# The second mixer of a two-layer trunk: gate rows read from masked tables in DRAM in place of broadcasts on TensorE

## The chip, the core and the metric

The kernel runs on one core of one Trainium2 chip. A core has TensorE (matrix products, rows PE, its weight loads PEld), VectorE (DVE), ScalarE (ACT), GpSimd (POOL), SyncE (SP, which here only issues transfers) and 16 DMA engines. Each engine works through its own instructions in a fixed order; semaphores tie them together. Products land in PSUM, everything else lies in SBUF, 128 partitions wide, or in DRAM. The metric is the device time of one execution in microseconds (us).

## The reference

Two layers of a bidirectional trunk run over 128 context tokens and 512 latent tokens, 1024 wide, with the same weights. The first layer mixes tokens by a gated delta rule and attention, the second by an mLSTM; each is followed by a gated feed-forward. The change is in the second mixer. Its recurrence, for each of 8 heads and both directions, is

```python
    log_d = jnp.where(incl, b[..., :, None] - b[..., None, :] + log_i[..., None, :], -jnp.inf)
    def step(carry, inp):
        m_t = jnp.maximum(m_in, m_intra_c)
        w_inter = jnp.exp(m_in - m_t)
        s = qk_c * jnp.exp(log_d_c - m_t[..., None])
        num = w_inter[..., None] * jnp.einsum('bhtk,bhkv->bhtv', q_c, C) + jnp.einsum('bhts,bhsv->bhtv', s, v_c)
        den = w_inter * jnp.einsum('bhtk,bhk->bht', q_c, nv) + jnp.sum(s, axis=-1)
        h = num / jnp.maximum(jnp.abs(den), jnp.exp(-m_t))[..., None]
```

What matters here: the exponent of `s` is a sum of a term of the key position s, a term of the query position t (call it the gate row, one value per t), and a mask that is 0 or very negative. `w_inter` is the exponential of another piece of the same gate row. Afterwards `h` is normalised, gated and multiplied by `ml_w_out`.

## The kernel before

All of it is one Tile program, `tile_trunk`. The 640 tokens are 5 tiles of 128. Products in fp32 are made of three passes over values split into a high and a low part; the weights come in by SP's transfers (`wr`), are cast on ScalarE (`wh`, L477) and the rest is made on VectorE (`wl`, L478). Thirty SBUF slots of 128 x 1296 are handed out in turn (`U.get`, `U.put`); a transfer into a slot waits until its last reader is done. `later` is a queue of deferred pieces of work, of which `tick(n)` runs n. The program's text gives the order only in outline: a scheduler decides at build time in which order each engine gets its instructions.

The second mixer, `layer1`, projects token by token in five chunks (`gemm_tok`, `in_w_ml`, to about 1098 us). Behind the first chunk `gates` makes, on a few partitions, `r2f`, the gate rows of 8 heads and 2 directions over 640 tokens, and their exponentials in partitions 64 to 127. Both are split into `r2h` (a cast, L1654) and `r2l` (the difference, L1655).

Then come ten units, in the order context unit 0, latent 0 to 3, context unit 1, latent 4 to 7. A latent unit is one head and four tiles of 128 tokens; a context unit is four heads and one tile. For each unit `weights` makes `qk` (L1743), and for each direction the exponent `bc` in PSUM: one product with the identity puts the mask there (L1749), and one each with `r2h` and `r2l` adds the gate row to all 128 partitions (L1754; four narrow ones each in a context unit). For latent units `qb` is the exponential row on all partitions (L1759, L1760), which VectorE multiplies into the queries (`mqs`, L1762). ScalarE takes four exponentials `me` of `bc` with the key's term `colA` as bias (L1766), and VectorE multiplies by `qk` (L1768). `outputs` makes `num` and `numb` from these (L1783, L1786), the normaliser `rn` on VectorE, `hs` in two halves (ScalarE L1803, VectorE L1805), squares `jk` on ScalarE (L1809) and the reciprocal root `mrs` on POOL (L154). `store` applies it (L1821), transposes on TensorE (`ht`, L1823) and splits the result. A unit's `weights` stand ahead of the `outputs` of the unit before. From unit 5 on the output projection `op` (L502) is laid between the units. Before the first unit's outputs come the state updates of all chunks (`ktok`, `wk`, `mst` L1718, `st` L1724).

Of the kernel before, what the change touches and what calls it, by code (L numbers as in the profile page):

```python
# [11 lines left out]
F32 = mybir.dt.float32  # L12
# [73 lines left out]
def tile_trunk(ctx: ExitStack, tc: tile.TileContext, A, dbg=None, stop=None):  # L86
# [402 lines left out]
    def tick(n=1):  # L489

        for _ in range(min(n, len(later))):
            later.popleft()()
# [32 lines left out]

    def gemm_tok(x, units, kk, n, evac, depth=3, fill=0, fills=None):

        ga, gb, mm_ = g_tile("tka"), g_tile("tkb"), m_tile("tkm")
        accs = [ga[:, 0:512], ga[:, 512:1024], gb[:, 0:512], gb[:, 512:1024], mm_[:, :]]
        for u in range(units):  # L530
# [18 lines left out]
            if u < units - 1:  # L549
                tick(2)  # L550

# [164 lines left out]
    def ffn_s(l, nm, xt, xs, xd, done):  # L716
# [27 lines left out]
        with tc.tile_pool(name=f"wp{l}", bufs=2, side="right") as rp:  # L744
# [38 lines left out]

            hid = {}

# [8 lines left out]
            for f in range(CLASSIC, NF, 2):  # L794
                last = f == NF - 2
                gate = None
                for which in range(2):
# [3 lines left out]
                    def then(n):  # L801
                        if end and n == 0:
                            W.until = len(wspecs) if l else w_layer1
                            W.fetch(2)
                        if end:
                            for _ in range(2):
                                if coming[0] < THIRDS[0][1]:
                                    hid_in(coming.popleft())
                        else:
                            step(STEPS[min(unit, 3)][n], todo)  # L810
                        if n == 5 and unit >= 3 and ada_todo:
                            ada_fill(1)
                            ada_load(1)
# [662 lines left out]


    def layer1(nm, xt, xs, xd):
        with ExitStack() as lay:
# [43 lines left out]

            gt = sm([NT, 32], "gt")
            vsl = [U.get("v1") for _ in range(4)]
# [28 lines left out]

            r2h, r2l = sm([T], "r2h", F32R), sm([T], "r2l", F32R)
            dec = sm([NT], "dec")
# [5 lines left out]
            def gates():  # L1562
                gls = U.get("gl")
                gl = gls[:, :1280].rearrange("p (t a r) -> p t a r", t=NT, a=4)
                pool.memset(gls[:, :1280], 0.0)
                fx, fa = sm([NT, 16], "fx"), sm([NT, 16], "fa")
                dve.tensor_tensor(out=fx, in0=gt[:, :, 16:32], in1=fb[:, None, :].to_broadcast([P, NT, 16]), op=ALU.add)
# [24 lines left out]
                for j in range(4):  # L1592
                    for d in range(2):
                        src = 1 + (j if d == 0 else 3 - j)
                        pe.matmul(pi[0:64, 512 + P * j:640 + P * j], lhsT=gl[:, src, 2 + d, :], rhs=sl[d][:, 896:1024],
                                  start=d == 0, stop=d == 1)
                U.put(gls, *sl)
                br = U.get("br")
# [54 lines left out]
                act.activation(br[64:128, 648:648 + T], br[0:64, 648:648 + T], AF.Exp)  # L1653
                act.copy(r2h, r2f)  # L1654
                dve.tensor_tensor(out=r2l, in0=r2f, in1=r2h.bitcast(F32), op=ALU.subtract)  # L1655
                act.activation(ra[64:128], ra[64:128], AF.Exp)
# [32 lines left out]
            for c in range(1, 5):  # L1689
                for i in sorted({hh // 2 for kind, hh, _, _ in ML_CHUNKS[c] if kind == "o"} - set(ogs)):  # L1690
                    ogs[i] = U.get("og")
                    ogv[i] = ogs[i][:, :1280].rearrange("p (t h d) -> p t h d", t=NT, h=2)
                gemm_tok(h, 4, 2, 416, evac(ML_CHUNKS[c]), 3, fill=1 if len(ada_todo) > 8 else 0)
                next(pieces, None)
                next(pieces, None)
            h.put()


# [39 lines left out]
            def weights(items):  # L1738
# [5 lines left out]
                hh = items[0][0]  # L1744
                bc = g_tile("bc")
                qs, ss = [], []
                for d in range(2):
                    bd = bc[:, 512 * d:512 * d + 512]
                    pe.matmul(bd, lhsT=ident_r, rhs=mneg_r[:, d, None, :].to_broadcast([P, 4, P]), start=True, stop=False)  # L1749
                    rows = [(hh, slice(0, 512), slice(TP, T))] if lat else [  # L1750
                        (h_, slice(i * P, i * P + P), slice(0, TP)) for i, (h_, c) in enumerate(items)]
                    for part in (r2h, r2l):
                        for i, (h_, o, src) in enumerate(rows):
                            pe.matmul(bd[:, o], lhsT=ident_r[:, 32 * d + h_:32 * d + h_ + 1].to_broadcast([P, P]),  # L1754
                                      rhs=part[:, src], start=False, stop=part is r2l and i == len(rows) - 1)
                    if lat:
                        qb = m_tile("qb")
                        row = ident_r[:, 64 + 32 * d + hh:65 + 32 * d + hh].to_broadcast([P, P])
                        pe.matmul(qb, lhsT=row, rhs=r2h[:, TP:T], start=True, stop=False)  # L1759
                        pe.matmul(qb, lhsT=row, rhs=r2l[:, TP:T], start=False, stop=True)  # L1760
                        q_ = t_tile("mqs")
                        dve.tensor_tensor(out=q_[:, :512], in0=qb, in1=qp[hh][:, TP:T], op=ALU.mult)  # L1762
                        qs.append(q_)
# [4 lines left out]
                    dve.tensor_tensor(out=e[:, :512], in0=e[:, :512], in1=pq, op=ALU.mult)  # L1768
                    ss.append(e)
                return qs, ss  # L1770

            def outputs(items, qs, ss):
# [73 lines left out]
            def finish(u):  # L1846
                store(order[u], *hss.pop(u))
                hh, c = order[u][0]
                if c and hh % 2:
                    U.put(vsl[hh // 2], ogs[hh // 2], qsl[hh // 2])  # L1850
                    if hh % 4 == 3:
                        U.put(ksl[hh // 4])

            wts[0] = weights(order[0])
            pt = ktok(0)
            wks = deque(wkeys(0, d, pt) for d in range(2))
            steps = [(1 + n if d == 0 else 4 - n, d, n) for n in range(3) for d in range(2)]
            for i in range(8):
# [11 lines left out]
                if i == 5:  # L1870
                    wts[1] = weights(order[1])
            U.put(cps)
            W.until = len(wspecs)
            for u in range(1, len(order)):
                if u + 1 < len(order):
                    wts[u + 1] = weights(order[u + 1])
                finish(u - 1)
                if u == 5:
# [174 lines left out]
```

## Time and profile before

| | us |
|---|---|
| runs | 1692.59, 1695.3, 1696.57 |
| median | 1695.3 |
| profiled execution | 1693.63 |
| its span in the profile | 1691.9 |
| TensorE busy | 1636.2 (97%) |
| VectorE busy | 1229.7 (73%) |
| ScalarE busy | 763.0 (45%) |

The span is what the trace covers; the execution's own time is 1.7 longer. An engine's busy time is the time in which it had an instruction under way, so a share of the span is an average over stages that have different limits. For TensorE the starts of successive matmuls tell more than their durations, which overlap. A wait is shown with what released the engine.

### The profile page before, as it was taken

What the parts mean: (1) busy time and instruction counts of PE and PEld (TensorE: products, weight loads), DVE (VectorE), ACT (ScalarE), POOL (GpSimd) and SP (SyncE); (2) the same over time, 40 slices, a digit from 0 to 9 for tenths busy, and PEclk for the clock granted to TensorE, in tenths of its full rate; (3) what the DMA queues carried; (4) which work ended last, traced back from release to release, by engine and by line L of the source; (5) the groups of instructions that cost most, each with busy time, mean ns of one, the idle gap of its engine ahead of it and who ended that gap; (6) DMA issues with size and microseconds to landing.
All of it is one profiled execution on the core that took longest, in us unless ns stands there. A gap on an engine that the chain in (4) does not pass through costs nothing. (4 is left out here: it accounts for less than half of the span.)

```text
span 1691.9 us, 28080 instructions
## 1 busy us (share of the span) xinstructions
PE 1636.2 (97%) x10896; PEld 1561.8 (92%) x10896; DVE 1229.7 (73%) x2354; ACT 763.0 (45%) x1646; POOL 149.6 (9%) x243
## 2 busy tenths in 40 slices
PE   7999988998999999999999999999999999999998
PEld 3799776798999999999999989978999999999998
DVE  7788977777888888978855755377677988865432
ACT  5784255564455444442224623246455534443210
POOL 0000024641000000000001000001010000000000
PEclk9999999999999999999999999999999999999999
DMA  8232611105621544467532434401240444338221
GB/s 337 92 101 83 198 45 29 29 13 161 233 90 66 169 148 158 147 212 276 202 99 98 155 88 158 151 28 57 92 164 24 137 167 142 118 109 308 88 76 63
DMA packets 80653, 216.21 MB, mean 128 GB/s; under 512 B 20196, under 2 KB 21348, under 8 KB 80520
## 3 DMA queue, kind: packets, MB, share of 16 engines
q1 hardware_dynamic: 75720, 194.75, 35.1%
q0 software_dynamic: 4800, 19.66, 3.0%
q8 instruction: 86, 1.41, 0.3%
q14 instruction: 47, 0.39, 0.1%
HBM read 186.85 MB, written 27.53 MB: 127 GB/s over the span
## 5 line engine op out<-in xcount | busy, mean ns | idle before, releaser
L502 PE MATMUL fd<-hid,wh 128*128 128x320 f32 x1408 | 264.5, 309 | 0.0
L477 ACT CAST wh<-wr 128x1024 fp32r<-128x1024 f32 (+4 forms) x148 | 134.1, 912 | 275.5 <-DMA wr<-in_w_d 131.6
L502 PEld LDWEIGHTS fd<-hid,wh 128*128 128x128 f32 x1408 | 220.9, 188 | 0.0
L692 PE MATMUL sb<-ht,ph 128*128 128x320 f32 x1008 | 199.3, 311 | 0.7 <-DVE ht L614 0.5
L478 DVE TENSOR_TENSOR wl<-wr,wh 128x1024 fp32r<-128x1024 f32 (+3 forms) x116 | 133.3, 1152 | 87.2 <-ACT wh L477 62.1
L692 PEld LDWEIGHTS sb<-ht,ph 128*128 128x128 f32 x1008 | 160.5, 188 | 3.0 <-DVE ht L614 0.8
L502 PE MATMUL fd<-hid,wl 128*128 128x320 f32 x704 | 160.2, 309 | 0.0
L318 DVE SCALAR_TENSOR_TENSOR aj<-ar,cs 128x1024 bf16<-128x1024 f32 x112 | 133.7, 1220 | 24.9 <-DMA ar<-in_ada_w 24.9
L692 PE MATMUL sad<-hb,ph 128*128 128x320 f32 x576 | 128.1, 309 | 0.0
L502 PEld LDWEIGHTS fd<-hid,wl 128*128 128x128 f32 x704 | 118.0, 188 | 0.0
L502 PE MATMUL op<-mxh,wh 128*128 128x320 f32 x512 | 99.0, 312 | 1.1 <-DVE xc L554 1.0
L554 DVE SCALAR_TENSOR_TENSOR xd<-fd,mod,xd 128x128 f32<-128x128 f32 x96 | 48.4, 546 | 66.6 <-PE fd L502 66.5
L692 PEld LDWEIGHTS sad<-hb,ph 128*128 128x128 f32 x576 | 96.4, 188 | 0.0
L652 DVE TENSOR_TENSOR pl<-s,ph 128x1024 fp32r<-128x1024 f32 x72 | 88.0, 1222 | 4.1 <-ACT ph L651 3.6
L692 PE MATMUL sad<-hb,pl 128*128 128x320 f32 x288 | 88.9, 309 | 0.0
L692 PE MATMUL sb<-ht,pl 128*128 128x320 f32 x288 | 88.7, 308 | 0.0
L651 ACT CAST ph<-s 128x1024 fp32r<-128x1024 f32 x72 | 75.2, 1049 | 27.3 <-PE fg L502 8.9
L502 PEld LDWEIGHTS op<-mxh,wh 128*128 128x128 f32 x512 | 80.9, 188 | 2.0 <-ACT rh L216 1.2
L651 ACT CAST ph<-wp 128x1024 fp32r<-128x1024 f32 (+1 forms) x72 | 60.0, 835 | 41.5 <-PE sad L692 22.8
L692 PE MATMUL sad<-ht,ph 128*128 128x320 f32 x288 | 64.9, 313 | 1.3 <-DVE c L703 1.1
L652 DVE TENSOR_TENSOR pl<-wp,ph 128x1024 fp32r<-128x1024 f32 x36 | 44.0, 1221 | 29.1 <-issue 21.1
L692 PE MATMUL sb<-hn,ph 128*128 128x320 f32 x288 | 64.8, 309 | 0.0
(551 smaller groups left out, 3997.1 us busy)
## 6 DMA issues: line engine op xcount, KB each, us to landing
ar<-in_ada_w SPq DMA_DIRECT2D x61, 512.0 KB
wp<-in_w_g SPq DMA_DIRECT2D x36, 512.0 KB
wp<-in_w_u SPq DMA_DIRECT2D x36, 512.0 KB
wr<-in_w_d SPq DMA_DIRECT2D x32, 512.0 KB
hf<-hd SPq DMA_DIRECT2D x44, 320.0 KB
hd<-c POOLq DMA_DIRECT2D x36, 320.0 KB, 2.5
adas<-in_ada_w SPq DMA_DIRECT2D x19, 512.0 KB
wr<-in_w_ml SPq DMA_DIRECT2D x20, 416.0 KB
```

The costliest lines, as they stand in the source:

```text
L318: dve.scalar_tensor_tensor(out=junk, in0=st, scalar=one, in1=ada["cs"][:, s, :], op0=ALU.mult, op1=ALU.mult, accum_out=mod[l][q][:, s, j:j ...
L477: act.copy(hi, raw[:, :n])
L478: dve.tensor_tensor(out=lo, in0=raw[:, :n], in1=hi.bitcast(F32), op=ALU.subtract)
L502: pe.matmul(ps[:, LO + a:LO + b], lhsT=wv[:, k, :], rhs=xk[:, a:b], start=k == 0 and p_ == 0, stop=k == kk - 1 and p_ == 2)
L554: dve.scalar_tensor_tensor(out=x[:, a:b], in0=ps[:, LO + a:LO + b], scalar=gate[:, s, j:j + 1], in1=x[:, a:b], op0=ALU.mult, op1=ALU.add)
L651: act.copy(hi, src)
L652: dve.tensor_tensor(out=lo, in0=src, in1=hi.bitcast(F32), op=ALU.subtract)
L692: pe.matmul(bank[o], lhsT=wv[:, k, :], rhs=xv, start=o not in seen and k == 0 and p_ == 0, stop=k == 3 and p_ == 2, skip_group_check=True)
```

## The change

A generator `masks` runs in the first feed-forward, at most one step in each of its units 3 to 14: it loads the mask once, spreads it over 128 x 1024 on VectorE and stores it into ten tables `mb` in DRAM, 512 KB each. In `gates` the split is gone; eight transfers on SP store the latent gate rows (`rl`), their exponentials (`re`) and the context rows (`rc`) in DRAM, and ten `add_row` are put on `later`: each is a transfer on POOL's queue that reads a row on all 128 partitions and adds it to a table in DRAM. `gemm_tok` takes one piece of `later` after each weight tile in the last four chunks where it took two. `weights` has no products for `bc` and `qb` left: the exponentials read the table from a slot `mbt`, the queries are multiplied by `qbt`, and `load_rows` brings both in, two units ahead. The small gate tiles move to a slot `gx`. Names in the new kernel: its L1743 is L1774, L1766 is L1786, L1783 and L1786 are L1816 and L1819.

```diff
@@ gemm_tok
-    def gemm_tok(x, units, kk, n, evac, depth=3, fill=0, fills=None):
+    def gemm_tok(x, units, kk, n, evac, depth=3, fill=0, fills=None, ticks=2):
...
-                tick(2)
+                tick(ticks)
@@ ffn_s
-            hid = {}
+            hid, masking = {}, masks()
...
+                        if n == 3 and l == 0 and 3 <= unit < 15:
+                            next(masking, None)
@@ new, ahead of layer1
+    def masks():
+
+        r = U.get("mrep")
+        m_ = v3(r[:, 1024:1280], 2)
+        sp.dma_start(out=m_, in_=A["mneg"])
+        dve.tensor_copy(r[:, :1024].rearrange("p (d c t) -> p d c t", d=2, c=4), m_.unsqueeze(2).to_broadcast([P, 2, 4, P]))
+        yield
+        for i in range(10):
+            mb.append(dram.tile([P, 2 * TS], F32, name=f"mb{i}"))
+            sp.dma_start(out=mb[i], in_=r[:, :1024])
+            yield
+        U.put(r)
+
@@ layer1, gates
-            r2h, r2l = sm([T], "r2h", F32R), sm([T], "r2l", F32R)
+            rl, re = (dram.tile([8, 2 * TS], F32, name=n) for n in ("rl", "re"))
+            rc = dram.tile([2, 2, 4, TP], F32, name="rc")
...
-                act.copy(r2h, r2f)
-                dve.tensor_tensor(out=r2l, in0=r2f, in1=r2h.bitcast(F32), op=ALU.subtract)
+                for d in range(2):
+                    r8, t_ = slice(32 * d, 32 * d + 8), slice(TS * d, TS * d + TS)
+                    sp.dma_start(out=rl[:, t_], in_=r2f[r8, TP:T])
+                    sp.dma_start(out=re[:, t_], in_=br[64 + 32 * d:72 + 32 * d, 648 + TP:648 + T])
+                    for g_ in range(2):
+                        sp.dma_start(out=rc[g_, d], in_=r2f[32 * d + 4 * g_:32 * d + 4 * g_ + 4, 0:TP])
+
+                def add_row(i):
+                    row = rl[i:i + 1, :] if i < 8 else rc[i - 8].rearrange("d i t -> (d i t)").unsqueeze(0)
+                    pool.dma_start(out=mb[i], in_=row.to_broadcast([P, 2 * TS]), accum_op=ALU.add)
+
+                later.extend(lambda i=i: add_row(i) for i in (8, 0, 1, 2, 3, 9, 4, 5, 6, 7))
@@ layer1, after the gates
-                gemm_tok(h, 4, 2, 416, evac(ML_CHUNKS[c]), 3, fill=1 if len(ada_todo) > 8 else 0)
+                gemm_tok(h, 4, 2, 416, evac(ML_CHUNKS[c]), 3, fill=1 if len(ada_todo) > 8 else 0, ticks=1)
...
             h.put()
+            tick(len(later))
@@ weights
-                bc = g_tile("bc")
+                mbt, qbt = rows.popleft()
                 qs, ss = [], []
                 for d in range(2):
-                    bd = bc[:, 512 * d:512 * d + 512]
-                    pe.matmul(bd, lhsT=ident_r, rhs=mneg_r[:, d, None, :].to_broadcast([P, 4, P]), start=True, stop=False)
-                    rows = [(hh, slice(0, 512), slice(TP, T))] if lat else [
-                        (h_, slice(i * P, i * P + P), slice(0, TP)) for i, (h_, c) in enumerate(items)]
-                    for part in (r2h, r2l):
-                        for i, (h_, o, src) in enumerate(rows):
-                            pe.matmul(bd[:, o], lhsT=ident_r[:, 32 * d + h_:32 * d + h_ + 1].to_broadcast([P, P]),
-                                      rhs=part[:, src], start=False, stop=part is r2l and i == len(rows) - 1)
+                    bd = mbt[:, TS * d:TS * d + TS]
                     if lat:
-                        qb = m_tile("qb")
-                        row = ident_r[:, 64 + 32 * d + hh:65 + 32 * d + hh].to_broadcast([P, P])
-                        pe.matmul(qb, lhsT=row, rhs=r2h[:, TP:T], start=True, stop=False)
-                        pe.matmul(qb, lhsT=row, rhs=r2l[:, TP:T], start=False, stop=True)
                         q_ = t_tile("mqs")
-                        dve.tensor_tensor(out=q_[:, :512], in0=qb, in1=qp[hh][:, TP:T], op=ALU.mult)
+                        dve.tensor_tensor(out=q_[:, :512], in0=qbt[:, TS * d:TS * d + TS], in1=qp[hh][:, TP:T], op=ALU.mult)
...
                     ss.append(e)
+                U.put(mbt)
                 return qs, ss
+            rows = deque()
+            def load_rows(items):
+                hh, c = items[0]
+                mbt, qbt = U.get("mb"), None
+                sp.dma_start(out=mbt[:, :2 * TS], in_=mb[hh if c else 8 + hh // 4])
+                if c:
+                    qbt = hq.tile([P, 2 * TS], F32, tag="qb", bufs=2, name="qb")
+                    sp.dma_start(out=qbt, in_=re[hh:hh + 1, :].to_broadcast([P, 2 * TS]))
+                rows.append((mbt, qbt))
 
@@ units
+            load_rows(order[0])
+            load_rows(order[1])
             wts[0] = weights(order[0])
...
                 if i == 5:
                     wts[1] = weights(order[1])
+                    load_rows(order[2])
...
                     wts[u + 1] = weights(order[u + 1])
+                if u + 2 < len(order):
+                    load_rows(order[u + 2])
```

What the scheduler made of it on three engines follows, of before and of the changed kernel.

TensorE, at one of the last latent units, behind a piece of the output projection (`wh`, `mxh` and `mxl` belong to it); before:

```order
L1743 MATMUL qk<-qp_9543,kp_10087 128x128 x4
L1749 MATMUL bc<-mneg_r,ident_r 128x512
L1754 MATMUL bc<-r2h,ident_r 128x512
L1754 MATMUL bc<-r2l,ident_r 128x512
L1759 MATMUL qb<-r2h,ident_r 128x512
L1760 MATMUL qb<-r2l,ident_r 128x512
L1759 MATMUL qb<-r2h,ident_r 128x512
L1760 MATMUL qb<-r2l,ident_r 128x512
L1783 MATMUL num<-v_573_9893,me 128x129
L1786 MATMUL num<-st_11164,mqs 128x129
```

and now:

```order
L502 MATMUL op<-mxh_680_11211,wh_12002 128x320 x2
L1774 MATMUL qk<-qp_9567,kp_10111 128x128 x4
L1816 MATMUL num<-v_576_9917,me 128x129
L1819 MATMUL num<-st_11202,mqs 128x129
L1816 MATMUL num<-v_576_9917,me 128x129
```

The seven products of the mask, the gate row and the exponential rows between `qk` and the first `num` are gone, and the three in the second direction too.

ScalarE, at the end of the projections (`og` are gate evacuations out of the accumulators `tkb`, `tkm`); before:

```order
L1548 ACTIVATE og_10817<-tkm 128x128
L1546 ACTIVATE og_11004<-tkm 128x256
L1548 ACTIVATE og_10414<-tkm 128x32
L1766 ACT_TABLE_LOAD
L1766 ACTIVATE me<-bc,colA 128x128 x8
L1721 COPY cp_11170<-mst 128x258 x4
```

and now, where `mb_11213` is the slot with the table of context unit 0:

```order
L1566 ACTIVATE og_10442<-tkb 128x32
L1786 ACT_TABLE_LOAD
L1786 ACTIVATE me<-mb_11213,colA 128x128
L1566 ACT_TABLE_LOAD
L1566 ACTIVATE og_10851<-tkb 128x128
L1564 ACTIVATE og_11041<-tkb 128x256
L1566 ACTIVATE og_10442<-tkb 128x32
L1566 ACTIVATE og_10851<-tkm 128x128
L1564 ACTIVATE og_11041<-tkm 128x256
L1566 ACTIVATE og_10442<-tkm 128x32
L1786 ACT_TABLE_LOAD
L1786 ACTIVATE me<-mb_11213,colA 128x128 x7
```

One exponential, which reads the loaded table, now stands ahead of the last six evacuations, with a load of the function table on either side; the seven others stand behind them, with a third.

POOL, behind the gates (`gl`, `br`, `cb` are tiles of the gates, `mrs` the reciprocal roots of the mixer); before:

```order
L1565 MEMSET gl_10144 128x1280
L1624 MEMSET br_10240 128x640
L1603 MEMSET cb_10242 64x64
L1603 MEMSET cb_10243 64x64
L1603 MEMSET cb_10244 64x64
L154 TENSOR_TENSOR mrs<-msq,mhalf 128x4 x10
```

and now, `mb8` and `mb9` being the tables of the context units and `mb0` to `mb7` those of the heads:

```order
L1623 MEMSET cb_604_10266 64x64
L1683 DMA mb8_7286<-rc_10105 128x1024
L1683 DMA mb9_7416<-rc_10105 128x1024
L1683 DMA mb0_6237<-rl_10103 128x1024
L1683 DMA mb1_6367<-rl_10103 128x1024
L1683 DMA mb2_6499<-rl_10103 128x1024
L1683 DMA mb3_6629<-rl_10103 128x1024
L1683 DMA mb4_6761<-rl_10103 128x1024
L1683 DMA mb5_6891<-rl_10103 128x1024
L1683 DMA mb6_7023<-rl_10103 128x1024
L1683 DMA mb7_7154<-rl_10103 128x1024
L154 TENSOR_TENSOR mrs_11362<-msq_11345,mhalf_87 128x4
```

The ten additions stand in a row on POOL's queue between the gates and the mixer. On SP seven of the ten stores of the masks stand in a row between two pairs of the first feed-forward's weight loads (`in_w_g`, `in_w_u`), three behind; and seven table loads stand where loads of the residual (`xc`) were, near the end of the projections.

## Rows read from the trace of the kernel before

**Rows 1.** The page, busy times of the engines and the granted clock in 40 slices

```profile
PE 1636.2 (97%) x10896; PEld 1561.8 (92%) x10896; DVE 1229.7 (73%) x2354; ACT 763.0 (45%) x1646; POOL 149.6 (9%) x243
...
PEclk9999999999999999999999999999999999999999
```

**Rows 2.** Windows: length; PE, PEld, DVE, ACT, POOL busy; clock; DMA share; GB/s

```profile
1098.10:1116.60 18.50, 17.48 (x172) 13.78 (x171) 11.52 (x34) 9.12 (x34) 0.10 (x1) 1.00 0.19 65
1116.60:1166.00 49.40, 45.02 (x333) 39.56 (x332) 36.92 (x111) 28.95 (x109) 4.94 (x5) 1.00 0.09 28
1166.00:1217.50 51.50, 51.50 (x374) 49.71 (x373) 37.38 (x110) 25.25 (x93) 5.34 (x5) 1.00 0.13 42
1217.50:1247.20 29.70, 28.71 (x193) 28.16 (x193) 22.68 (x43) 16.56 (x27) 3.66 (x7) 1.00 0.74 257
```

**Rows 3.** Waits from 1116.6 to 1166.0 us: total us, times, longest

```profile
ACT me L1766 <- PE bc L1754: 13.0, 6, 3.9
PEld num L1783 <- ACT jk L1809: 4.1, 4, 1.7
ACT hs L1803 <- DVE rn L1797: 3.8, 4, 1.5
```

**Rows 4.** Timeline of PE, first matmuls of two units: start, us, what

```profile
1128.99 1.06 PE L1743 MATMUL qk<-qp,kp 128*128 128x128 f32 x8
...
1137.10 1.05 PE L1743 MATMUL qk<-qp,kp 128*128 128x128 f32 x8
```

**Rows 5.** Timeline of PE, around the gate rows of a latent unit

```profile
1166.81 0.48 PE L1749 MATMUL bc<-mneg_r,ident_r 128*128 128x512 f32 x1
...
1168.52 0.38 PE L1783 MATMUL num<-v,me 128*128 128x129 f32 x2
...
1169.77 0.47 PE L1749 MATMUL bc<-mneg_r,ident_r 128*128 128x512 f32 x1
...
1170.54 0.38 PE L1783 MATMUL num<-v,me 128*128 128x129 f32 x2
```

**Rows 6.** Timeline of PE, a direction of the first context unit

```profile
1098.93 0.47 PE L1749 MATMUL bc<-mneg_r,ident_r 128*128 128x512 f32 x1
...
1100.09 1.06 PE L1731 MATMUL ktok<-cm,kp 128*128 128x128 f32 x8
```

**Rows 7.** Timeline of ACT, the first exponentials of the mixer

```profile
1099.32 1.28 ACT L1766 ACT_TABLE_LOAD   x1
1100.61 1.14 ACT L1766 ACTIVATE me<-bc,colA 128x128 f32<-128x128 f32 x4
```

**Rows 8.** Timeline of DVE in the gates

```profile
1007.66 0.83 DVE L1655 TENSOR_TENSOR r2l<-br,r2h 128x640 fp32r<-128x640 f32 x1 [2.01 <-ACT r2h L1654]
...
1009.52 1.22 DVE L318 SCALAR_TENSOR_TENSOR aj<-ar,cs 128x1024 bf16<-128x1024 f32 x1
```

**Rows 9.** SP's DMA issues in the first feed-forward

```profile
569.31 1.73 SPq L635 DMA_DIRECT2D wp<-in_w_g  x2
...
586.55 0.80 SPq L635 DMA_DIRECT2D wp<-in_w_u  x2
```

**Rows 10.** Windows, columns as in group 2

```profile
560.00:575.00 15.00, 15.00 (x103) 14.95 (x103) 9.45 (x12) 7.44 (x12) 0.00 (x0) 1.00 0.48 155
1010.00:1030.00 20.00, 20.00 (x117) 19.20 (x116) 14.38 (x22) 8.56 (x23) 0.00 (x0) 1.00 0.60 191
1030.00:1060.00 30.00, 29.43 (x156) 28.76 (x155) 16.89 (x30) 7.44 (x20) 0.00 (x0) 1.00 0.42 133
1080.00:1098.00 18.00, 18.00 (x94) 17.15 (x94) 1.02 (x1) 2.71 (x10) 0.00 (x0) 1.00 0.51 164
1220.00:1230.00 10.00, 10.00 (x69) 9.84 (x69) 7.45 (x15) 5.84 (x11) 1.14 (x2) 1.00 1.01 356
```

**Rows 11.** POOL: the page's issues (KB, us to landing)

```profile
hd<-c POOLq DMA_DIRECT2D x36, 320.0 KB, 2.5
```

**Rows 12.** Timeline of POOL, its first instruction after the gates

```profile
1116.50 1.01 POOL L154 TENSOR_TENSOR mrs<-msq,mhalf 128x4 f32<-128x4 f32 x1 [138.05 <-DVE msq L1811]
```

More of the change, by code (lines that the diff above doesn't have):

```diff
@@ L1475, in layer0 @@
         return mx
+    mb = []
+    def masks():
[9 more added lines that the diff above has]
+        U.put(r)
     def layer1(nm, xt, xs, xd):
@@ L1521, in layer1 @@
             U.put(nm.bc)
-            gt = sm([NT, 32], "gt")
+            gx = U.get("gx")
+            gt, fx, fa = (gx[:, a:b].rearrange("p (t h) -> p t h", t=NT) for a, b in ((0, 160), (160, 240), (240, 320)))
             vsl = [U.get("v1") for _ in range(4)]
@@ L1565, in gates @@
                 pool.memset(gls[:, :1280], 0.0)
-                fx, fa = sm([NT, 16], "fx"), sm([NT, 16], "fa")
                 dve.tensor_tensor(out=fx, in0=gt[:, :, 16:32], in1=fb[:, None, :].to_broadcast([P, NT, 16]), op=ALU.add)
@@ L1596, in gates @@
                                   start=d == 0, stop=d == 1)
-                U.put(gls, *sl)
+                U.put(gls, gx, *sl)
                 br = U.get("br")
```

## The prediction

> **What bounds the kernel now.** I read the busy shares and the slices first [rows 1]. TensorE is busy for 97% of the span, VectorE for 73%, ScalarE for 45%, and TensorE's clock is granted in full in all forty slices, so nothing here is to be won or lost by the clock. The second mixer runs from 1098 to 1247 us. I read it in stages, since a mean hides that its stages have different limits [rows 2]. The reader is to compare TensorE's busy time with the length of each stretch. In the last one of the scan, 1166.0 to 1217.5 (three latent units, with the output projection between them), TensorE is busy for 51.50 of 51.50 us: work taken from it there shortens the stage one for one, until the next engine, VectorE with 37.38, is full. In 1116.6 to 1166.0 TensorE still has 45.02 of 49.4 us, but VectorE has 36.92, and the units go round a loop of three engines: ScalarE's exponentials wait 13.0 us there for the broadcasts on TensorE, TensorE's weight loads wait for ScalarE, ScalarE for VectorE [rows 3]. In 1098.1 to 1116.6 (first context unit, state updates) nothing is full.
>
> **What is taken off TensorE.** In a latent unit the first direction spends 1166.81 to 1168.52 on the mask, the gate row's two halves and the two exponential rows, the second 1169.77 to 1170.54 [rows 5]. Starts are subtracted, since the rows' durations overlap: 1.71 + 0.77 = 2.48 us a unit, and 8 units make 19.8. In a context unit a direction spends 1098.93 to 1100.09 = 1.16 us [rows 6]; two units of two directions make 4.6. Together 24.5 us. Of the 24.5, three latent units lie in 1166.0 to 1217.5 (7.4); the first context unit lies in 1098.1 to 1116.6 (2.3; with the first pieces of the latent unit behind it some 3.6, an estimate); about 13.5 remain for 1116.6 to 1166.0.
>
> **What that is worth, stage by stage.**
> - 1166.0 to 1217.5: TensorE would fall from 51.5 to 44.1 and still lead VectorE's 37.4. The whole 7.4 could come off. But ScalarE's casts and VectorE's differences then stand closer to TensorE, and TensorE's order still has the short dependent pieces of each unit; I take 6, bounds 0 and 7.4.
> - 1116.6 to 1166.0: VectorE's 36.92 is a floor, so no more than 12.5 can come off. Its multiplications stay: the exponential-row product keeps its size and reads SBUF where it read PSUM. The rest of the loop (normaliser, two scalings, the square sum, the reciprocal root on POOL, transposes) keeps its length, and only the 13.0 us in which ScalarE waited for the broadcasts can go. The likely next wait is ScalarE for VectorE and back. I take half of 12.5, 6.2; bounds 0 and 12.5.
> - 1098.1 to 1116.6: TensorE gives back 3.6. Against it stands ScalarE's new order: the first exponential now stands ahead of the last six gate evacuations, and the table of functions is loaded three times where it was loaded once. A load took 1.28 us, and the next activation began at its end, 1100.61 [rows 7]; two more are 2.6. The first exponential also waits for the 512 KB of its table, and behind it on ScalarE are evacuations that free TensorE's PSUM. I take 0, bounds 3 earlier and 3 later.
>
> On the table load the Trainium skill (ScalarE: Activation LUTs, What ACT_TABLE_LOAD costs) counts 1.28 us for the load and about 1.4 us more of drain. Here the 1.28 agrees and no drain shows behind it; by the page the two extra switches would be 5.3 us and the time about 2.7 later.
>
> - Output projection's end, 1217.5 to 1247.2: TensorE has 28.71 of 29.70 us and the DMA engines are at 0.74 [rows 2]; it asks for the same bytes as before. I take 0.
> - In gates, a cast on ScalarE and VectorE's 0.83 us difference of the gate rows [rows 8] go, far ahead of the mixer, where TensorE works on the projections; worth 0.
>
> **What is added.** The masks: one load, one VectorE copy of 128 x 1024 (about 1.2 us, by a VectorE piece of that width [rows 8]), ten stores of 512 KB in the first feed-forward. VectorE there has 9.45 of 15.00 us, the DMA engines are busy for 0.48 at 155 GB/s [rows 10]. Seven stores stand in a row on SP between two weight loads issued at 569.31 and 586.55 [rows 9]. The highest rate that a stretch of this profile shows is 356 GB/s with the engines at 1.01 [rows 10], so 201 GB/s are left beside the 155, and the seven stores (3.7 MB) take 18 us of it, one more than the 17 between those issues; the other three (1.6 MB) another 8. If the weights behind them are late by all of that, it costs 9; if they have the slack, 0. TensorE is full there, with nothing late in the rows, and the two loads prepare a later step; I take 0.5.
>
> The rows: eight small stores on SP, then ten additions on POOL's queue, each of which makes 512 KB out of a row and adds it to 512 KB in DRAM. POOL is idle for 138 us there [rows 12], so nothing queued on it waits. In the order they stand in a row with nothing between them but landings, so they run as one burst from about 1007, and not one by one through the chunks as the code reads. No row shows an accumulating transfer to DRAM. The nearest is POOL's store of 320 KB, which lands 2.5 us after its issue [rows 11]: scaled to 512 KB it is 4 us, and three such passes (row, table, result) are 12 us, both estimates. Ten of them take 40 to 120 us if they follow each other, and the first table is wanted 92 us after 1007, the others about every 8 (two units' first matmuls stand at 1128.99 and 1137.10 [rows 4]). So the tables should be there. What they take from the weight loads in 1010 to 1098 is 0 to 16 (below); I take 0.5.
>
> The loads: 512 KB of table and, for a latent unit, 512 KB of row broadcast. Seven tables are asked for before 1098, where context tiles were, and the DMA engines were busy for 0.51 of 1080 to 1098 [rows 10]; the rest lies in stretches at 0.09 and 0.13 [rows 2]. Each is asked for two units ahead, some 16 us; 1 MB at 356 GB/s is 3 us. Price 0; if that cover is gone at the start, it is the 3 of the first stage's bound.
>
> **The sum.** 1693.6 (the profiled execution, 1.7 above its span) - 6 - 6.2 - 0 + 0.5 + 0.5 = 1682.4. The median of the runs shown lies 1.7 above the profiled one, so the forecast for a median is 1684.
>
> **The rivals.**
> 1. All that TensorE loses comes off: 7.4 + 12.5 + 3 = 22.9, and nothing is lost elsewhere: 1695.3 - 22.9 = 1672. For: TensorE leads in three of four stages. Against: the loop's floor on VectorE would have to be met without a gap.
> 2. The gain is hidden. The loop waits as long for ScalarE and VectorE as it did for the broadcasts, and two extra table loads and the wait for the first table come on top: -6 in the last stage, 0 in the loop, +3 at the start, and +1 for the DMAs: 1693. For: the rows of waits show short waits in a ring. Against: 13.0 us of them are for broadcasts alone.
> 3. Slower. The burst of additions shares the 16 DMA engines with the mixer's weights from 1010 to 1060, where TensorE is busy for 20.00 of 20 us and the engines already for 0.60 and 0.42 [rows 10]. The weights of these 50 us are 0.191 x 20 + 0.133 x 30 = 7.8 MB, which at 356 GB/s is 22 us, an estimate. The additions are 5.2 MB; if each byte costs a read of the row, a read of the table and a write, 15.7 MB, 44 us more: 66 in 50, and TensorE starves for 16. It decides at about 28 us for the additions, two passes a byte: then they still fit. The time would be 1684 + 16 = 1700. Or each addition takes over 18 us, and the later tables are late by the same mechanism.
>
> The Trainium skill (DMA: Bandwidth & Descriptors, Issuing engines are not separate DMA queues) says that transfers run on the same 16 engines and interleave whoever issued them, so POOL's queue being idle would not keep the additions out of the weights' way. No row before shows the two together; by that rule the result is 1700 rather than 1684 if the additions are as heavy as in rival 3.
>
> That the change doesn't do what it says is excluded for TensorE: the order has no broadcast left.
>
> **How the numbers follow.** The forecast (1678 to 1690) gets 0.48, the full gain 0.14, the hidden gain 0.18, the starved weights 0.20. 1684 is the likeliest. A measurement of this kernel can tell about 0.2% (3.4 us) from no change, so faster is below 1691.9 and slower above 1698.7. Faster: 0.48 + 0.14 + a quarter of the hidden case = 0.67; same 0.13; slower 0.20. The range 1672 to 1699 leaves out half of each outer case, about 0.2.
>
> **What would show it.** Right: TensorE full and shorter by 6 in the last stage; the loop's units nearer 7 than 8.1 us; no wait for tables on ScalarE beyond the first; additions landing by 1090. Wrong: ScalarE idle on a table load for more than 5 us, TensorE idle between 1010 and 1098 on weights, the ffn's weights late at about 590, or a clock below full in the stage that got gaps.

## The result, and the profile after

The changed kernel takes 1703.17 us (median of 6 runs, 1701.87 to 1708.61), the kernel before 1695.83 (6 runs): a ratio of 1.0051, 95% interval 1.0036 to 1.0065. It is slower by about 7.3 us, beyond the range of the prediction and on the side of its third rival. The profiled execution of the changed kernel is the longest of its six (1708.61, span 1706.8); the one of before is among the shortest (1693.63), so the 14.9 us between the two spans are more than the change. A second trace of the changed kernel is among the experiments.

The page of the changed kernel, busy times and granted clock (as in [rows 1]):

```profile
PE 1627.8 (95%) x10780; PEld 1559.5 (91%) x10780; DVE 1226.7 (72%) x2354; ACT 765.5 (45%) x1647; POOL 159.6 (9%) x253
...
PEclk9999999999999999999999998998999999999999
```

TensorE's busy time is 8 us less, though 24 us of matmuls are gone; it is busy for 95% where it was 97%, and two slices have a clock under 0.9 where none had. The stretches show where. First the projections of the second mixer in the kernel before, then in the changed kernel the projections, the loop, the units with the output projection, and that projection's end (columns as in [rows 2]):

```profile
1002.30:1098.10 95.80, 95.23 (x508) 92.05 (x507) 49.45 (x79) 30.41 (x79) 0.00 (x0) 1.00 0.52 161
```

```profile
1003.80:1116.90 113.10, 103.74 (x509) 99.05 (x508) 48.67 (x78) 31.17 (x80) 8.48 (x10) 0.91 0.69 194
...
1136.80:1182.70 45.90, 35.59 (x266) 33.12 (x265) 36.64 (x112) 30.29 (x114) 5.06 (x5) 0.89 0.43 147
1182.70:1229.50 46.80, 44.99 (x342) 44.11 (x341) 35.59 (x106) 24.59 (x91) 5.04 (x5) 1.00 0.23 74
1229.50:1262.60 33.10, 30.46 (x198) 30.01 (x197) 24.23 (x47) 17.42 (x29) 3.91 (x7) 0.95 0.66 228
```

The projections have the same TensorE work and the same weights in both kernels. They take 113.1 us where they took 95.8, with the clock granted at 0.91 in the mean. In the loop TensorE's busy time fell from 45.02 of 49.40 [rows 2] to 35.59 of 45.90: the matmuls are gone, but the stretch shortened by 3.5 us only, and VectorE's 36.64 is close to its 36.92 of before.

The same stages in the other traces, cut at starts of matmuls in each trace (the chunks' first `tka`; the first `qk` of units 1, 2 and 8; the last group of `ht`; the first `fg` of the feed-forward), in us. By these cuts the last units of before end 1.1 us earlier than in the window of [rows 2]:

| kernel | start | projections | first unit, states | loop | last units | end |
|---|---|---|---|---|---|---|
| before | 1002.3 | 95.8 | 18.5 | 49.4 | 50.4 | 30.7 |
| changed | 1003.8 | 113.1 | 19.9 | 45.9 | 46.8 | 33.1 |
| changed, second trace (e12) | 999.3 | 112.8 | 19.9 | 45.6 | 46.8 | 30.8 |
| e1, no additions | 1003.2 | 97.0 | 19.9 | 45.9 | 47.0 | 30.4 |
| e2, additions spread | 1001.4 | 116.8 | 21.3 | 45.6 | 46.5 | 30.2 |
| e3, before with masks and additions | 999.8 | 105.6 | 18.5 | 50.3 | 50.4 | 31.1 |
| e4, before with masks | 1002.3 | 95.6 | 18.5 | 50.0 | 50.4 | 31.0 |
| e5, e1 with ScalarE's order kept | 1001.7 | 95.8 | 16.6 | 44.3 | 46.9 | 30.4 |
| e6, mask added by POOL in SBUF | 1003.8 | 96.0 | 16.6 | 44.0 | 50.9 | 30.4 |
| e7, half-size additions | 999.9 | 109.2 | 19.9 | 45.9 | 46.5 | 31.1 |
| e8, mixer without its loads | 1002.8 | 97.5 | 20.7 | 44.7 | 48.5 | 30.7 |
| e9, additions in the mixer | 1001.5 | 103.3 | 18.2 | 49.8 | 47.1 | 32.2 |
| e10, e6 with rows three ahead | 1003.6 | 95.8 | 16.6 | 50.7 | 45.1 | 30.5 |
| e11, exponential rows late | 1000.6 | 108.9 | 19.9 | 45.6 | 46.9 | 30.9 |

The column of starts shows how far executions differ in work that no kernel here changes but for the masks: 999.3 to 1003.8. The projections repeat far better in the two traces of the changed kernel (113.1 and 112.8; the end does not, 33.1 and 30.8), so causes are read from stages and verdicts from the runs.

What happens in the projections: POOL, idle there before [rows 12], issues its ten additions in two groups (timeline of POOL, the changed kernel: start, us, what, idle before), and the second view is the DMA queue of those additions and their median time to landing between 995 and 1075 us:

```profile
1004.97 1.82 POOL L1683 DMA_DIRECT2D mb<-rc  x2 [24.73 <-DMA rc<-br]
1017.02 6.66 POOL L1683 DMA_DIRECT2D mb<-rl  x8 [10.23 <-DMA rl<-br]
```

```profile
q0 software_dynamic: 1440, 5.24, 34.4%
...
mb<-rl POOLq DMA_DIRECT2D x8, 512.0 KB, 21.0
mb<-rc POOLq DMA_DIRECT2D x2, 512.0 KB, 10.0
```

The queue took 34.4% of 80 us on 16 engines, 27.5 us of all of them for 5.24 MB. In the kernel before, a weight asked for in this stage is cast about 4 us later (SP's issue, ScalarE's cast):

```profile
1026.48 0.33 SPq L471 DMA_DIRECT2D wr<-in_w_ml  x1
```

```profile
1030.56 0.89 ACT L477 CAST wh<-wr 128x832 fp32r<-128x832 f32 x1 [2.05 <-DMA wr<-in_w_ml]
```

In the changed kernel, while the additions run, SP issues two weights (first view), ScalarE casts them (second), and TensorE waits (third: the two longest of its waits there):

```profile
1021.40 0.33 SPq L471 DMA_DIRECT2D wr<-in_w_ml  x1
...
1024.62 0.33 SPq L471 DMA_DIRECT2D wr<-in_w_ml  x1
```

```profile
1030.37 0.88 ACT L477 CAST wh<-wr 128x832 fp32r<-128x832 f32 x1 [9.19 <-DMA wr<-in_w_ml]
...
1031.70 1.28 ACT L1566 ACT_TABLE_LOAD   x1
1033.00 0.20 ACT L1566 ACTIVATE og<-tka 128x32 f32<-128x32 f32 x1
```

```profile
1018.20 0.72 PE L539 MATMUL tka<-wl,hh 128*128 128x416 f32 x1 [2.49 <-DVE wl L478]
...
1033.25 0.71 PE L539 MATMUL tka<-wh,hh 128*128 128x416 f32 x1 [4.57 <-ACT og L1566]
```

The weight asked for at 1021.40 is cast at 1030.37, 9.0 us later, where the kernel before took 4.1 (and 3.3 for another, 1065.93 to 1069.18). ScalarE works in order: the cast stands ahead of the evacuations `v` and `og` of the chunk that is ending, these read the accumulators `tka` into which TensorE's next matmuls write, and so TensorE waits 4.57 us for `og`, not for the weight. The other wait, 2.49 us, goes by VectorE, where the low part `wl` of a weight is made late:

```profile
1017.12 1.03 DVE L478 TENSOR_TENSOR wl<-wr,wh 128x832 fp32r<-128x832 f32 x1 [5.10 <-DMA ar<-in_ada_w]
```

The profile puts its 5.10 us of idle time down to a load of `ar`, the other stream that SP brings in during this stage. In the kernel before no `wl` waits for `ar`. So it is not only the weights that come late. Then the clock. Windows of the changed kernel:

```profile
1010.00:1020.00 10.00, 7.51 (x36) 7.01 (x35) 4.90 (x8) 0.89 (x1) 2.98 (x6) 0.91 0.99 265
1020.00:1030.00 10.00, 8.68 (x42) 8.20 (x41) 6.97 (x12) 0.89 (x1) 3.68 (x5) 0.92 1.04 258
1030.00:1040.00 10.00, 5.28 (x16) 4.55 (x17) 2.65 (x3) 5.83 (x18) 0.00 (x0) 0.59 1.05 271
1040.00:1050.00 10.00, 10.00 (x42) 9.36 (x41) 2.38 (x4) 2.04 (x4) 0.00 (x0) 0.56 1.01 247
1040.00:1045.00 5.00, 5.00 (x25) 4.55 (x24) 0.00 (x0) 1.27 (x3) 0.00 (x0) 0.50 1.05 264
```

Of these 40 us TensorE is idle for 8.5 (2.49 + 1.32 + 4.72). It is granted 0.91, 0.92, 0.59 and 0.56; busy time times what is lacking of the full clock is, as an estimate, 0.7 + 0.7 + 2.2 + 4.4 = 8.0 us. Together 16.5 of the 17.3 that the projections lost. In 1040 to 1045 TensorE has no idle time at all and stands at 0.50, the lower of its two levels (1.2 GHz of 2.4), after the idle time between 1028.7 and 1039.3.

### The profile page after: what moved, and what is told of

Its sections match the earlier page's. It is cut to its first block, busy times and chain, and to the rows that moved or that the text cites. A ratio compares the mean times of both kernels' runs of the same rounds, so it can differ in the third digit from the quotient of the medians.

```text
span 1706.8 us, 27908 instructions
## 1 busy us (share of the span) xinstructions
PE 1627.8 (95%) x10780; PEld 1559.5 (91%) x10780; DVE 1226.7 (72%) x2354; ACT 765.5 (45%) x1647; POOL 159.6 (9%) x253
## 5 line engine op out<-in xcount | busy, mean ns | idle before, releaser
L502 PE MATMUL op<-mxl,wh 128*128 128x320 f32 x256 | 60.2, 316 | 0.0
```

Source lines behind the costliest of these rows:

```text
L502: pe.matmul(ps[:, LO + a:LO + b], lhsT=wv[:, k, :], rhs=xk[:, a:b], start=k == 0 and p_ == 0, stop=k == kk - 1 and p_ == 2)
```

## The experiments

**e1, the additions left out.**

```diff
                 def add_row(i):
                     row = ...
-                    pool.dma_start(out=mb[i], in_=row.to_broadcast([P, 2 * TS]), accum_op=ALU.add)
+                    pass
```

> The changed kernel with the ten additions of gate rows left out (the tables hold the mask alone, so the mixer's weights are not the reference's). Theory A, that the burst of additions starves the weights in the projections and the rest follows from it: the projection stretch is back to about 96 us from 113, TensorE's clock is full there, and the time is 17 to 18 us below the changed kernel's, about 1685. Theory B, that the mixer's own new traffic and order are what costs: the projections gain little, and the time stays above 1695.

1686.2 us against 1695.68 of before, ratio 0.9945 [0.9933, 0.9957]. The projections and the loop:

```profile
1003.20:1100.20 97.00, 95.31 (x508) 92.14 (x508) 48.52 (x78) 31.17 (x80) 0.00 (x0) 1.00 0.53 172
...
1120.10:1166.00 45.90, 35.62 (x267) 33.13 (x266) 36.61 (x112) 30.33 (x114) 5.04 (x5) 0.89 0.45 147
```

The projections are back at 97.0 with a full clock: theory A. The additions cost 17 us, more than the whole of what the rest of the change gains, 9.5.

**e2, one addition to a weight tile.**

```diff
-                    pool.dma_start(out=mb[i], in_=row.to_broadcast([P, 2 * TS]), accum_op=ALU.add)
+                    q_ = pool.dma_start(out=mb[i], in_=row.to_broadcast([P, 2 * TS]), accum_op=ALU.add)
+                    tc.add_manual_dep(q_.ins, mark[0].ins.name, ...)   (mark: the last matmul of the tile)
```

> The changed kernel with each addition tied to the last matmul of one weight tile of the projections, one addition to a tile, so that they are spread over some 60 us in place of about 40. Theory A in the form that the burst matters, not the bytes: the additions' 27 us of the engines fit beside the weights' 22, TensorE is idle less than 2 us in the projections, clock full, time about 1686. Rival, that their bytes in any order take the weights' place: TensorE is idle in the projections as before the spreading, above 6 us, time about 1700.

1709.49 us, ratio 1.0077 [1.0055, 1.0099]: no faster than the burst, whose interval it meets, and by the projections (116.8 us) slower. TensorE's idle time is the rival's, but neither line foresaw this size. One place shows why: the addition on POOL, the weight on SP 0.3 us later, and its cast and the evacuations behind it on ScalarE:

```profile
1079.03 0.81 POOL L1685 DMA_DIRECT2D mb<-rl  x1 [4.88 <-PE tkm L541]
```

```profile
1079.33 0.33 SPq L471 DMA_DIRECT2D wr<-in_w_ml  x1
```

```profile
1086.97 0.88 ACT L477 CAST wh<-wr 128x832 fp32r<-128x832 f32 x1 [8.73 <-DMA wr<-in_w_ml]
1087.77 0.38 ACT L1566 ACTIVATE og<-tka 128x256 f32<-128x256 f32 x1
```

The end of a weight tile is when the addition is released and also when the next weight is asked for. That weight is cast 7.6 us after its issue, at the end of a chunk, with `og` behind it. Such a collision came at three ends of chunks, and TensorE waited 15.0 us in all for `og`. So this run spreads the additions, but releases each at the moment at which a weight is asked for; what spreading alone would do it does not tell.

**e3, the kernel before with masks, row stores and additions; e4, with the masks alone.** The mixer is that of before in both; e4 adds the generator `masks` and its call in the feed-forward, e3 also this:

```diff
+                for d in range(2):
+                    (stores of rl, re, rc)
+                later.extend(lambda i=i: add_row(i) for i in (8, 0, 1, 2, 3, 9, 4, 5, 6, 7))
                 act.copy(r2h, r2f)
```

> The kernel before with the masks, the row stores and the ten additions added, and its mixer as it was (the tables are never read). Theory A: the projections lose the 17 us as in the changed kernel, with the same clock loss: about 1713. Theory B: under 1700.

> The kernel before with only the masks added: the load, the copy and ten stores in the first feed-forward. Both theories: no more than 1 us above the kernel before, since TensorE had no idle time there in the changed kernel. A loss of 3 or more would say that the first feed-forward pays too.

e3: 1705.51, ratio 1.0056 [1.0044, 1.0068]; e4: 1694.35, ratio 0.999 [0.9982, 0.9999]. The additions lose time without the new mixer, 9.8 us of projections, fewer than the 17 expected; e11 has a part of the rest. Windows of e3, where TensorE is idle for 5.9 of 20 us while the additions run, and e4 while seven mask stores move (SP's issue, then the window):

```profile
1010.00:1020.00 10.00, 7.93 (x34) 7.42 (x34) 7.12 (x10) 1.78 (x2) 6.66 (x8) 0.83 1.05 301
1020.00:1030.00 10.00, 6.22 (x29) 5.75 (x28) 4.37 (x8) 4.64 (x12) 0.00 (x0) 0.88 1.06 250
```

```profile
573.96 4.84 SPq L1491 DMA_DIRECT2D mb<-mrep  x7
```

```profile
575.00:590.00 15.00, 15.00 (x105) 15.00 (x103) 12.61 (x19) 6.40 (x10) 1.07 (x2) 1.00 0.99 369
```

In e4 the DMA engines are full, 369 GB/s at 0.99, a little above the highest rate of before [rows 10], and TensorE has no idle time: the weights in the feed-forward stand a burst. The masks cost nothing.

**e5, ScalarE's order.** The run without additions, and

```diff
-                        act.activation(e[:, i * P:i * P + P], bd[...], AF.Exp, bias=colA[...])
+                        ex = act.activation(e[:, i * P:i * P + P], bd[...], AF.Exp, bias=colA[...])
+                        if not wts:
+                            tc.keep_in_program_order(ex)
```

> The run without additions (additions left out, as there), and in addition the first unit's exponentials kept behind the last gate evacuations on ScalarE, so that the function table is loaded once there. Theory: the first stage of the mixer, 19.9 us from its first qk to the next unit's, falls by the two loads and the evacuations' wait, to 16 to 17, and the time to about 1683 from 1686. Rival, that the stage is bound by the state updates' chain: within 1 us of 1686.

1685.49, ratio 0.994 [0.9923, 0.9957]. ScalarE at the first exponentials, the changed kernel and then e5, whose order is that of before [rows 7]:

```profile
1115.41 1.28 ACT L1786 ACT_TABLE_LOAD   x1
1116.71 0.40 ACT L1786 ACTIVATE me<-mb,colA 128x128 f32<-128x128 f32 x1
1117.11 1.28 ACT L1566 ACT_TABLE_LOAD   x1
1118.41 0.28 ACT L1566 ACTIVATE og<-tkb 128x128 f32<-128x128 f32 x1
...
1119.60 1.28 ACT L1786 ACT_TABLE_LOAD   x1
1120.90 2.15 ACT L1786 ACTIVATE me<-mb,colA 128x128 f32<-128x128 f32 x7
```

```profile
1098.76 1.28 ACT L1786 ACT_TABLE_LOAD   x1
1100.05 2.44 ACT L1786 ACTIVATE me<-mb,colA 128x128 f32<-128x128 f32 x8
```

The first unit's stage fell from 19.9 to 16.6 us, as expected; the runs (1681.6 to 1688.4) don't tell it from e1's 1686.2. So the stage is settled and the gain in the end is not.

**e6, no additions in DRAM.** Each row is read on all partitions into the slot, and POOL adds the mask there; masks, tables and `add_row` are gone, and ScalarE's order is kept as in e5:

```diff
-                sp.dma_start(out=mbt[:, :2 * TS], in_=mb[hh if c else 8 + hh // 4])
+                row = rl[hh:hh + 1, :] if c else rc[hh // 4].rearrange("d i t -> (d i t)").unsqueeze(0)
+                sp.dma_start(out=mbt[:, :2 * TS], in_=row.to_broadcast([P, 2 * TS]))
+                for d in range(2):
+                    pool.tensor_tensor(out=v3(mbt[:, TS * d:TS * d + TS], 4), in0=v3(mbt[:, TS * d:TS * d + TS], 4),
+                                       in1=mneg_r.bitcast(F32)[:, d, None, :].to_broadcast([P, 4, P]), op=ALU.add)
```

> The changed kernel with neither tables in DRAM nor additions there: each unit's row is read on all partitions from DRAM into the slot, and POOL, idle there, adds the mask in SBUF; the first exponentials stay behind the gate evacuations. Theory A, that the DRAM additions are the only loss: 1682 to 1686, below both kernels. Rival: POOL's additions (some 2.7 us each half unit by the rate of its 128 x 252 pieces) or the port they share with VectorE come into the units' loop: 1690 or more.

1689.08, ratio 0.996 [0.9945, 0.9976]: below both kernels, but between the two lines, 1682 to 1686 and 1690 or more. The windows of e6 (projections, loop, last units), and one pair of POOL's additions:

```profile
1003.80:1099.70 95.90, 95.45 (x507) 92.05 (x507) 48.66 (x78) 29.67 (x78) 7.39 (x6) 1.00 0.54 174
...
1116.30:1160.30 44.00, 32.79 (x267) 30.11 (x265) 37.32 (x111) 29.83 (x112) 7.61 (x7) 0.96 0.46 149
1160.30:1211.20 50.90, 47.30 (x342) 45.72 (x341) 38.89 (x111) 25.04 (x91) 10.60 (x9) 0.97 0.21 72
```

```profile
1124.76 2.55 POOL L1781 TENSOR_TENSOR mb<-mb,mneg_r 128x512 f32<-128x512 f32 x2 [7.04 <-DMA mb<-rl]
```

The projections have a full clock, and the loop is the shortest of all; POOL needs 1.3 us for a half unit, half of what was estimated. The last units take 50.9 us, as long as before the change (50.4).

**e7, half-size additions.** One direction of two:

```diff
-                    pool.dma_start(out=mb[i], in_=row.to_broadcast([P, 2 * TS]), accum_op=ALU.add)
+                    pool.dma_start(out=mb[i][:, :TS], in_=row[:, :TS].to_broadcast([P, TS]), accum_op=ALU.add)
```

> The changed kernel with each addition cut to one direction, 256 KB for 512 (the other direction's rows are left out). If the loss goes by the engines' time that is over (a threshold, 28 us by the prediction), half the additions, 14 us, fit beside the weights and the time is that without additions, about 1686. If every addition delays the weights that it meets, the loss is about half: 1693 to 1697.

1703.02, ratio 1.0033 [1.002, 1.0046]. Neither line: half the bytes leave 12 of the 16 us in the projections (against e1's 97.0). The additions' queue (995 to 1075) and TensorE's two waits of over 1 us in the burst:

```profile
q0 software_dynamic: 1440, 2.62, 20.3%
```

```profile
1012.84 0.46 PE L539 MATMUL tka<-wl,hh 128*128 128x416 f32 x1 [1.10 <-DVE wl L478]
...
1030.45 0.72 PE L539 MATMUL tka<-wh,hh 128*128 128x416 f32 x1 [8.62 <-ACT og L1566]
```

20.3% of 80 us is 16.2 us of the engines for 2.62 MB, where twice the bytes took 27.5. One collision at the end of a chunk, 8.62 us, makes most of the loss. There the last thing that the cast ahead of `og` waited for is VectorE's `aj`, which itself had waited for a load of `ar` (first VectorE, then ScalarE):

```profile
1025.14 1.23 DVE L318 SCALAR_TENSOR_TENSOR aj<-ar,cs 128x1024 bf16<-128x1024 f32 x1 [3.15 <-DMA ar<-in_ada_w]
```

```profile
1027.58 0.88 ACT L477 CAST wh<-wr 128x832 fp32r<-128x832 f32 x1 [7.79 <-DVE aj L318]
```

The additions' packets still ran until about 1029 (the DMA engines' share from 1005 to 1028 is 1.07), and the chunk's matmuls had come to this point at 1021.8. So what the additions cost in these runs depends on which load they meet, and on what stands behind it, more than on their sum.

**e8, the mixer without its loads.** The run without additions, and all units read one table and one exponential row that stay:

```diff
+                if not fixed:
+                    (one table and one row are loaded)
+                mbt, qbt = fixed
```

> The run without additions, and all units read one table and one exponential row that stay in SBUF (the rows of the other units are left out): the mixer without its new loads. If the loads are hidden, as the prediction says: within 1 us of the run without additions, 1686. If they delay the residual and the output projection's weights: 2 to 4 lower.

1686.81, ratio 0.9947 [0.9928, 0.9966], the same as e1's 0.9945. The mixer's loads are hidden.

**e9, the additions in the mixer.** Three in the projections, seven at the units, on the tie of e2:

```diff
+                if c >= 2:
+                    later.append(lambda i=(8, 0, 1)[c - 2]: adds[0](i))
...
+                if u + 4 < len(order):
+                    n = order[u + 4][0]
+                    adds[0](n[0] if n[1] else 8 + n[0] // 4)
```

> The changed kernel with three of the ten additions in the projections, one to each of the last three chunks, and seven in the mixer, one to a unit, where the DMA engines are at 0.04 to 0.15 in the kernel before; the first exponentials stay behind the gate evacuations. Theory A, that an addition costs only where just-in-time weights are loaded: the projections lose 0 to 5 us where they lost 17, the mixer's stages are as in the run without additions and with that order (16.6, 44.3, 46.9), and the time is 1685 to 1691. Rival, that an addition of 8 us in front of each table's load makes the tables late: the loop is longer than 47 us.

1694.14, ratio 0.9985 [0.9975, 0.9996]: better than the changed kernel, short of theory A. Three additions cost the projections 7.5 us, 2.5 each, and the loop is 49.8 us where e5 has 44.3: the rival's size, with the exponential row late where it named the table. VectorE waits for a late exponential row, and TensorE for VectorE:

```profile
1140.29 0.69 DVE L1789 TENSOR_TENSOR mqs<-qb,qp 128x512 f32<-128x512 f32 x1 [3.02 <-DMA qb<-re]
```

```profile
1142.62 0.47 PE L1865 MATMUL ht<-cm,hs 128*128 128x128 f32 x1 [4.85 <-DVE hs L1863]
```

**e10, rows three units ahead.** e6, with `load_rows` for unit u + 3 in place of u + 2 (the exponential rows as before):

> The variant in which POOL adds the mask in SBUF, with the rows asked for three units ahead in place of two. If its last stage, 50.9 us there against 46.9 in the run without additions, is long because a row is late: 46.9 again and 1685. If not: 1689 as there.

1691.84, ratio 0.9963 [0.9948, 0.9977], the same as e6. The last units fell to 45.1 us and the loop rose to 50.7. The 50.9 hung on when the rows are asked for, but the time has only moved; what holds the loop now stays open.

**e11, the first exponential rows held until the last chunk.**

```diff
+                    if not rows or len(rows) == 1 and not wts:
+                        tc.add_manual_dep(q_.ins, mark[1].ins.name, ...)   (q_: the load of the row)
```

> The changed kernel with the first loads of exponential rows, which fell into the burst at 1017 and 1022, held until the last chunk of the projections. If these two loads make up the difference between the changed kernel's projections (113) and those of the kernel before with the additions alone (105.6): 106 and about 1697. If not, 113 and 1703.

1699.43, ratio 1.0019 [1.0009, 1.0028]. The two loads, 1 MB that fell into the burst, are worth 3.9 of the projections' 113 and 4.2 us of the time; the expected 106 was too much. TensorE's waits in the projections:

```profile
PE tka L541 <- ACT og L1570: 4.6, 3, 3.3
PE tka L541 <- DVE wl L478: 2.9, 1, 2.9
```

**e12, the changed kernel again.**

> The changed kernel once more, for a second trace of it and a ratio on the same chip as the three others. By every theory: projections 113 us, clock below full between 1015 and 1050, 1703.

1703.61, ratio 1.004 [1.0026, 1.0053]. TensorE waits 5.0 us for `og` and 2.5 us for `wl` there, as in the first trace.

The sum of the parts, by medians: additions +9.8 (e3), the rows that fall into their burst +4.2 (e11), the rest of the change -9.5 (e1). That is +4.5 of the +7.3; the projections have some 3 us more, 108.9 in e11 against 105.6 in e3. Those 3 us are the clock's: TensorE is idle for 7.5 us in the one and 7.3 in the other, but busy for 101.50 at 0.94 against 98.35 at 0.97. Why it fell for longer with the same idle time stays open.

## Why the prediction was wrong, point by point

- **The additions, taken at 0.5 us.** This is the step that failed: they cost 17 us (e1). Its bounds, 0 to 16, held the 17 nearly, and the third rival named the place, the victim and the time, 1700; I gave it 0.20. I weighed it by capacity: weights 22 us and additions up to 44 in 50. The additions took 27.5 us of the engines, just under the 28 from which I let the rival decide, and TensorE still stood idle, with half of them too (e7). That the rival's 16 is so near is luck: it comes from 66 us of the engines' time in 50, where about 50 were needed, and it does not price the clock, which is about half of the loss. The sum over 50 us hides that the engines are full while the burst runs (0.99 to 1.05 in the windows from 1010 to 1050, where before had 0.60 and 0.42 [rows 10]). What decides shows in the trace of before: a weight is cast 3 to 4 us after its issue, and the next one is asked for only when a slot is free. With so short a lead, what counts is how long a load takes among others, 9 us in place of 4, and what stands behind its first reader.
- **"Nothing here is to be won or lost by the clock."** Wrong, though "a clock below full in the stage that got gaps" stood among my signs. Idle time of 8.5 us brought the clock down, and that cost about as much again, 8.0 us. It fell in the mixer as well: 0.89 in the loop, where TensorE has longer gaps now. I also misread the slices: a 9 stands for 0.9 or more, and the clock of before is full only from about 423 us on (two slices before that have 0.92).
- **Which rule held.** The Trainium skill (DMA: Bandwidth & Descriptors, Issuing engines are not separate DMA queues) says that transfers of all issuers interleave on the same 16 engines. The trace agrees: SP's weights went from 4 to 9 us while POOL's queue ran. I cited it and let the sum go by POOL's idle queue.
- **The last units, -6.** -3.6 measured (46.8 for 50.4), in e1 -3.4. Mechanism right, size off: TensorE has 44.99 of 46.80 and is no longer full to the last.
- **The loop, -6.2.** -3.5 measured. VectorE's work is as predicted, 36.92 before and 36.64 after. That the ring of waits takes the gain over was the second rival; half was too much. That the clock of 0.89 has a part in it is likely, but no run separates it.
- **The first unit, 0.** +1.4 measured, inside the bounds. ScalarE's new order is the cause: e5 takes 3.3 us back by keeping the old one, with one load in place of three. The price of a load was right: the next activations begin 1.30 us after each load's start (1115.41 to 1116.71, 1117.11 to 1118.41). The drain of about 1.4 us that the Trainium skill (ScalarE: Activation LUTs, What ACT_TABLE_LOAD costs) adds to a load does not show here; the measured 1.30 decides.
- **Masks at 0.5, mixer's loads at 0.** Right (e4, e8), with the exception of the two exponential rows that were issued early and fell into the burst (e11): I followed the table loads in the order, not these.
- **The rest of the change.** Without the additions it gains 9.5 us by the runs, against the 12.2 of the sum. From the mixer's start to the feed-forward the traces give 5.8 (149.0 and 143.2), and the projections lose 1.2 of it. The rest is that the profiled execution of e1 (1689.11) lies 2.9 us above its median and that of before about 2 below.
- **"The additions land by 1090."** They landed by about 1050; tables were never the matter.

## What to carry to other kernels

Before a transfer is put into a stage that is full on TensorE, read how long the stage's loads have from issue to use, and what stands behind their first reader on its engine; a share of 0.5 on the DMA engines was no room here, where each load has 4 us. Look for an idle engine that can do the work in SBUF before sending it by way of DRAM: here the kernel with POOL's additions in SBUF (e6, which also keeps ScalarE's order) took 1689 us and the one with additions in DRAM 1703. And ask of a gap on TensorE what it does to the clock: 8.5 us of idle time in 40 cost about 8 us more, while the 4.4 us in the loop of before, in short pieces, left the clock at 1.00 [rows 2].

## What the runs showed of the hardware

An addition of 512 KB onto DRAM lands 7 to 10 us after its issue when about two are under way (medians of 7.1 in e9 and 8.0 in e2, 10.0 for the first two of the changed kernel), and 21 us among eight; 5.24 MB of them take 27.5 us of all 16 engines, 191 GB/s, where the same engines moved 369 GB/s while plain stores and weights ran (e4). Half-size additions take 59% of that, not half. POOL adds two operands of 128 x 512 in fp32 in SBUF in 1.3 us (e6).
